# A two-stream encoder on one core: the last trailing chains on single PSUM banks, the sample's residual kept on chip through layer 1, and attention's turns cut differently

## The chip, the core and the metric

The kernel runs on one core of a Trainium2 chip. The core has a matrix engine (TensorE, PE in the profile), three element-wise engines (VectorE, DVE; ScalarE, ACT; GpSimd, POOL) and a queue that issues most transfers (SyncE, SP). TensorE writes its results into PSUM, eight banks of 128 partitions by 512 float32; the other operands lie in SBUF. The metric is device time of one execution in microseconds (us); lower is better.

## The reference

Two requests, the prompt (1024 tokens) and the sample (512 tokens), go through the same two layers of width 1024. Layer 0 mixes tokens with a grouped Fourier transform and a matrix, layer 1 with grouped-query attention (8 heads of 128, 2 key heads) with RMS-normed and rotated queries and keys. Each is followed by a SwiGLU of width 2816, and every step adds to a residual:

```python
for i in range(DEPTH):
    if i % 2 == 0:
        x = x + fourier_mixer(x, norm_mix[i], fourier_w[j])
    else:
        x = x + attention_mixer(x, norm_mix[i], attn_w_qkv[j], attn_q_norm[j],
                                attn_k_norm[j], attn_w_o[j], cos, sin)
    x = x + swiglu_ffn(x, norm_ffn[i], w_gate[i], w_up[i], w_down[i])
```

## The kernel before

**Blocks and precision.** Tokens stand in three blocks of 512: block 0 is the sample, blocks 1 and 2 the prompt. A residual block is eight tiles of 128 features by 512 tokens. Every product of two matrices is made of three matmuls (high by high, high by low, low by high part): `mm3`, lines 249 to 251, and `split` (lines 242 to 246) makes the two parts, a copy on ACT and a subtraction on DVE or POOL. One `mm3` on 512 columns is called a product below.

**Stages.** (1) The sample's Fourier layer. (2) The sample's SwiGLU of layer 0, woven with the prompt's Fourier layer. (3) `ffn_pair`: the prompt's SwiGLU of layer 0, both blocks at once in Strassen's manner. Behind its last round stand its trailing down products, which are issued in turns with the beginning of `main_1`. (4) `weave`: `main_1` (the sample's qkv, attention, out projection, norm and SwiGLU of layer 1) against `aux_2` (the prompt's qkv for block 2 and then block 1, its attention, its out projections, and `moving`, which prepares the operands of the last stage). (5) `ffn_pair` of layer 1, whose results go to the output `y`; its last trailing down products have nothing beside them.

**What sets the order.** The stages are Python generators. A `yield` carries a cost, and `weave` always continues the stream whose sum of costs, divided by its total, is smaller; so the costs only decide how two streams' instructions are mixed when they are written down. The Tile framework then schedules the written program with its own model of the engines and fixes one order for each engine and for the SP queue. On the chip each of them is first in, first out, and waits on semaphores.

**The trailing chains.** `product(k, d, f0)` (line 1034 on) is one product of the down matrix: `k` counts the seven Strassen products, `d` four output tiles. Four PSUM chains, one for each `d`, take products 0 to 3, then 4 and 5, then 6. After every product DVE adds the chain's running value to an accumulator (line 1054), so a chain's next product has to wait until that add has read the bank. In all rounds but the last a chain is one bank, from `bank()` or `bankg()`. In the last round (`f0 + 2 == NF`) of either layer it is one half of a tile of two banks (tag `gT`), which chains 0 and 1 share, and 2 and 3. The gate and up products of the same round use the same two `gT` tiles, one for each Strassen operand (`times`, line 1111 on).

**Sample's residual.** `accumulators()` takes two of the four 8 KB slots of the pool `accp`. In layer 1 the out projection (`linear_residual`, lines 744 to 755) loads a tile of the residual from DRAM into a temporary, adds the projection (line 752) and writes the sum back to DRAM (line 332). `normed` reads the eight tiles again (line 366), multiplies by the inverse norm on DVE (line 369) and splits them. `ffn` reads them a third time into accumulators it takes for itself (line 777). The prompt's attention uses the same pool: its transposed probabilities (`pt`) take two slots for a pair of query chunks.

**Attention.** `attend` goes over heads. For a query chunk `qc` of 128: `scores` (products into a `gX` tile, of which there is one, DVE's maximum on line 1346, ACT's exponential and scaling on lines 1350 and 1352); `turned` (eight transposes on PE, line 1364, split into `pt`); after every second chunk `values` (24 matmuls of 256 columns from `pt`). The prompt has eight chunks in a head, the sample four. The generator's yields stand between these steps.

Of the kernel before, what the change touches and what calls it, by code (L numbers as in the profile page):

```python
# [26 lines left out]
NF = DFF // P  # L27
# [98 lines left out]
def trunk_kernel(ctx: ExitStack, tc: tile.TileContext, t: dict):  # L126
# [59 lines left out]
    def tmp(n=TB, dt=F32):  # L186
        return tl("t", [n], dt, "t" + cur[0])
# [134 lines left out]
    def accumulators():  # L322
        halves = [acc_tile("acc", [4, TB], F32) for _ in range(2)]
        return [a[:, i] for a in halves for i in range(4)]
# [419 lines left out]
    def linear_residual(src, u, b, prev):  # L744

        for n in range(NC):
            w = weights(src[n])
            x = tmp()
            sp.dma_start(x, prev[:, n, :])
            ps = bank()  # L750
            project(w, u, ps)
            dve.tensor_tensor(x, ps, x, op=ALU.add)
            new_residual(b, n, x)
            yield 5.5


    kept, pend = {}, []

    def ffn(layer, b, h, out=None):
        h = h()  # L760
        here = b in resident
        acc = resident.pop(b) if here else accumulators()
        kept[b] = acc
        yield 0.0

        def halves(ms, wds, f0, dc):

            box = []

            def half(i):  # L770
                w = wds[dc // 4].rearrange("p h (f c) n -> p h f c n", f=2)
                mm3(box[0], w[:, 0, i, dc % 4], w[:, 1, i, dc % 4], ms[i][:, 0], ms[i][:, 1], i == 0, i == 1)

            def begin():
                box.append(bank())
                if f0 == 0 and not here:
                    sp.dma_start(acc[dc], xres[b][:, dc, :])
                half(0)

            def end():  # L780
                half(1)
                dve.tensor_tensor(acc[dc], box[0], acc[dc], op=ALU.add)  # L782
                if f0 + 2 == NF:
                    new_residual(b, dc, acc[dc], None if out is None else out[:, dc, :])

            return begin, end
# [135 lines left out]
    def ffn_pair(layer, blocks, ring, places, outs):  # L922
# [111 lines left out]
        def product(k, d, f0):  # L1034
# [8 lines left out]
            b, dc = blocks[c], 4 * o + d  # L1043
            acc = accs[b][dc]
            fresh, closes = k in (0, 4, 6), k in (3, 5, 6)
            if fresh and f0 + 2 < NF:
                chain[d] = bank() if d % 2 else bankg()
            elif fresh and d % 2 == 0:
                g2 = tl("a", [2, TB], F32, "gT", gt)
                chain[d], chain[d + 1] = g2[:, 0], g2[:, 1]  # L1050
# [254 lines left out]
    def attend(blocks, straight, slot):  # L1305
# [6 lines left out]
        for g in range(NKV):  # L1312
# [15 lines left out]
            for h in range(g * GROUP, (g + 1) * GROUP):  # L1328
# [49 lines left out]
                    act.copy(o, po[:, 0:256])  # L1378
                    sp.dma_start(dot[blocks[n]][:, h, c0 : c0 + 256], o)

                last = None
                for qc in range(nk + 1):
                    p = scores(qc) if qc < nk else None
                    yield 0.7 * nb
                    if qc:
                        turned(qc - 1, last)
                        yield 0.8 * nb
                        if qc % 2 == 0:
                            values(qc // 2 - 1)
                            yield 0.8 * nb  # L1390
                    last = p


    def weave(main, main_cost, aux=None, aux_cost=1.0, lead=0):
# [11 lines left out]
                runs.remove(run)  # L1406
        cur[0] = "F"

    FFN_US, PAIR_US, CHAIN_US, PROMPT_US = 352.0, 678.0, 223.0, 630.0

    mpt = open_pool("mp")
# [60 lines left out]

    def prepare(b, layer):

        yield from normed(b, g_ffn[layer], nxt, "A")

    def h_next():
        return nxt["h"]
# [49 lines left out]
    def out_projection(b, slot):  # L1528
        got = {}
        if b in mixed:  # L1530
            got["h"] = mixed.pop(b)
        else:
            yield from reloaded(dot[b], got, slot)
        yield from linear_residual(t["wo"], got["h"], b, xres[b])
# [6 lines left out]
    def main_1():  # L1541
        yield from qkv(0)
        yield from attend((0,), 0, "A")
        yield from out_projection(0, "A")
        yield from prepare(0, 1)
        yield from ffn(1, 0, h_next, t["y"][0])
# [128 lines left out]
```

## Time and profile before

| what | value |
|---|---|
| median of 3 runs | 2969.23 us (2968.76 to 2973.36) |
| the profiled execution: its time, its span | 2965.4 us, 2963.6 us |
| busy: PE, DVE, ACT, POOL | 2855.9, 1713.3, 1304.9, 1517.6 us |
| mean granted clock of TensorE | 0.99 |
| HBM read and written | 426.21 MB and 68.16 MB |
| direct transfers on SP's queue | 489.65 MB |

The profile is of one execution, and its times are counted from the span's start. A matmul's record is longer than its share of the pipeline: the pace of PE is read from one start to the next, not from a record's length. In a view of groups or of the timeline, a bracket or the part after the bar tells how long the engine had been idle before an instruction and which instruction of which engine ended the wait; PEld is the load of a matmul's stationary operand. "PEclk" is the clock that TensorE was granted, as a share of the full one.

### The profile page before, as it was taken

What the parts mean: (1) busy time and instruction counts of PE and PEld (TensorE: products, weight loads), DVE (VectorE), ACT (ScalarE), POOL (GpSimd) and SP (SyncE); (2) the same over time, 40 slices, a digit from 0 to 9 for tenths busy, and PEclk for the clock granted to TensorE, in tenths of its full rate; (3) what the DMA queues carried; (4) which work ended last, traced back from release to release, by engine and by line L of the source; (5) the groups of instructions that cost most, each with busy time, mean ns of one, the idle gap of its engine ahead of it and who ended that gap; (6) DMA issues with size and microseconds to landing.
All of it is one profiled execution on the core that took longest, in us unless ns stands there. A gap on an engine that the chain in (4) does not pass through costs nothing. (4 is left out here: it accounts for less than half of the span.)

```text
span 2963.6 us, 37198 instructions
## 1 busy us (share of the span) xinstructions
PE 2855.9 (96%) x13656; PEld 2350.0 (79%) x13656; DVE 1713.3 (58%) x3031; ACT 1304.9 (44%) x2131; POOL 1517.6 (51%) x932
## 2 busy tenths in 40 slices
PE   7999999999999999998998999999998999999998
PEld 6778878788888887786777888878886788888886
DVE  6674553566666667737646555552244466666666
ACT  5543232333333333646756776663333333333332
POOL 4344264766776774522241122224535767766763
PEclk8999999999999999999999999999999999999999
DMA  7435374766556553632242121115447865565552
GB/s 227 143 116 183 131 270 167 291 218 222 192 186 219 199 175 130 213 93 85 83 150 89 59 91 54 54 57 192 151 168 278 309 235 200 176 219 201 192 195 89
DMA packets 182326, 496.82 MB, mean 168 GB/s; under 512 B 19872, under 2 KB 30112, under 8 KB 180736
## 3 DMA queue, kind: packets, MB, share of 16 engines
q1 hardware_dynamic: 181216, 489.65, 48.5%
q0 software_dynamic: 640, 3.74, 0.4%
q8 instruction: 108, 1.77, 0.2%
q10 hardware_dynamic: 288, 1.05, 0.1%
q14 instruction: 74, 0.61, 0.1%
HBM read 426.21 MB, written 68.16 MB: 167 GB/s over the span
## 5 line engine op out<-in xcount | busy, mean ns | idle before, releaser
L288 POOL TENSOR_TENSOR w<-raw,w 128x1024 fp32r<-128x1024 f32 x200 | 479.0, 2402 | 843.9 <-ACT w L287 832.7
L243 POOL TENSOR_TENSOR w<-raw,w 128x512 fp32r<-128x512 f32 (+1 forms) x464 | 608.3, 1331 | 451.2 <-ACT w L242 445.0
L242 ACT CAST w<-raw 128x512 fp32r<-128x512 f32 (+1 forms) x464 | 279.6, 632 | 538.3 <-PE a L251 173.2
L287 ACT CAST w<-raw 128x1024 fp32r<-128x1024 f32 x200 | 208.7, 1049 | 269.5 <-PE g L251 77.9
L249 PE MATMUL g<-h,w 128*128 128x512 f32 x704 | 279.3, 397 | 9.9 <-ACT w L287 3.4
L251 PE MATMUL g<-h,w 128*128 128x512 f32 x704 | 277.8, 395 | 2.2 <-POOL w L288 2.2
L249 PE MATMUL a<-ring,w 128*128 128x512 f32 x712 | 279.5, 392 | 0.1
L251 PE MATMUL a<-ring,w 128*128 128x512 f32 x712 | 277.5, 390 | 0.0
L250 PE MATMUL a<-ring,w 128*128 128x512 f32 x712 | 277.3, 389 | 0.0
L250 PE MATMUL g<-h,w 128*128 128x512 f32 x704 | 276.8, 393 | 0.0
L1054 DVE TENSOR_TENSOR acc<-g,acc 128x512 f32<-128x512 f32 x280 | 192.5, 687 | 106.9 <-PE g L251 106.6
L1054 DVE TENSOR_TENSOR acc<-c,acc 128x512 f32<-128x512 f32 x280 | 192.4, 687 | 93.7 <-PE c L251 92.1
L249 PE MATMUL c<-mid,w 128*128 128x512 f32 x592 | 232.4, 393 | 13.3 <-ACT mid L242 7.6
L250 PE MATMUL c<-mid,w 128*128 128x512 f32 x592 | 232.6, 393 | 1.2 <-DVE mid L243 1.1
L251 PE MATMUL c<-mid,w 128*128 128x512 f32 x592 | 232.5, 393 | 1.3 <-POOL w L288 1.3
L249 PE MATMUL c<-h,w 128*128 128x512 f32 x480 | 191.5, 400 | 4.3 <-ACT h L245 3.3
L782 DVE TENSOR_TENSOR acc<-c,acc 128x512 f32<-128x512 f32 x176 | 120.9, 688 | 129.2 <-PE c L251 126.5
L250 PE MATMUL c<-h,w 128*128 128x512 f32 x480 | 189.1, 395 | 1.2 <-DVE h L246 0.9
L251 PE MATMUL c<-h,w 128*128 128x512 f32 x480 | 188.9, 394 | 0.0
L249 PEld LDWEIGHTS g<-h,w 128*128 128x128 f32 x704 | 133.0, 189 | 37.1 <-ACT w L287 3.8
L249 PEld LDWEIGHTS a<-ring,w 128*128 128x128 f32 x712 | 133.8, 188 | 33.8 <-DVE mid L243 4.4
L251 PEld LDWEIGHTS g<-h,w 128*128 128x128 f32 x704 | 132.9, 189 | 30.0 <-POOL w L288 3.3
(392 smaller groups left out, 6718.5 us busy)
## 6 DMA issues: line engine op xcount, KB each, us to landing
ring<-mov_B SPq DMA_DIRECT2D x248, 512.0 KB, 5.5
ring<-mov_T SPq DMA_DIRECT2D x88, 512.0 KB, 5.1
raw<-in_gate_dram SPq DMA_DIRECT2D x44, 512.0 KB, 3.6
raw<-in_up_dram SPq DMA_DIRECT2D x44, 512.0 KB, 3.5
raw<-in_down_dram SPq DMA_DIRECT2D x88, 256.0 KB, 3.1
raw<-in_gate_dram SPq DMA_DIRECT2D x88, 256.0 KB, 5.0
raw<-in_up_dram SPq DMA_DIRECT2D x88, 256.0 KB, 5.4
raw<-in_down_dram SPq DMA_DIRECT2D x44, 512.0 KB, 4.1
```

The costliest lines, as they stand in the source:

```text
L242: keep(act.copy(hi, src))
L243: keep(eng.tensor_tensor(lo, src, hi.bitcast(F32), op=ALU.subtract))
L249: pe.matmul(out, lh, rh, start=first, stop=False, **kw)
L250: pe.matmul(out, lh, rl, start=False, stop=False, **kw)
L251: pe.matmul(out, ll, rh, start=False, stop=last, **kw)
L287: pinned(act.copy(flat[:, 0], raw)) if early else act.copy(flat[:, 0], raw)
L288: pool.tensor_tensor(flat[:, 1], raw, flat[:, 0].bitcast(F32), op=ALU.subtract)
L782: dve.tensor_tensor(acc[dc], box[0], acc[dc], op=ALU.add)
L1054: dve.tensor_tensor(acc, chain[d], acc, op=ALU.add)
```

## The change

Three things are changed.

1. In the last round of layer 1, where `outs` is given, `product` takes single banks for its chains, as in the other rounds. Layer 0's last round keeps the `gT` halves, since the other stream is using the single banks by then.
2. `staying[0] = accumulators()` is taken before the sample's out projection. The residual is loaded straight into these tiles, stays there, is not written back, is read from there by `normed`, and is the accumulator of `ffn`. Eight writes (line 332) and sixteen reads (lines 366 and 777) of 256 KB leave SP's queue; the eight reads of line 749 remain. No engine other than SP has an instruction more or less.
3. `attend` yields at other places. The last turn of a head, which issues no scores, no longer yields 0.7. After the transposes of an even chunk it yields 2.0 (before 0.8), after those of an odd chunk 0.2 (before 0.8), after the values 0.2 (before 0.8), all times the number of blocks.

```diff
--- before.py
+++ after.py
@@ -745,21 +745,21 @@
 
         for n in range(NC):
             w = weights(src[n])
-            x = tmp()
+            x = staying[b][n] if b in staying else tmp()
             sp.dma_start(x, prev[:, n, :])
             ps = bank()
             project(w, u, ps)
             dve.tensor_tensor(x, ps, x, op=ALU.add)
-            new_residual(b, n, x)
+            new_residual(b, n, x, stays=b in staying)
             yield 5.5
 
 
-    kept, pend = {}, []
+    kept, pend, staying = {}, [], {}
 
     def ffn(layer, b, h, out=None):
         h = h()
         here = b in resident
-        acc = resident.pop(b) if here else accumulators()
+        acc = resident.pop(b) if here else staying[b]
         kept[b] = acc
         yield 0.0
 
@@ -773,8 +773,6 @@
 
             def begin():
                 box.append(bank())
-                if f0 == 0 and not here:
-                    sp.dma_start(acc[dc], xres[b][:, dc, :])
                 half(0)
 
             def end():
@@ -1043,7 +1041,7 @@
             b, dc = blocks[c], 4 * o + d
             acc = accs[b][dc]
             fresh, closes = k in (0, 4, 6), k in (3, 5, 6)
-            if fresh and f0 + 2 < NF:
+            if fresh and (f0 + 2 < NF or outs is not None):
                 chain[d] = bank() if d % 2 else bankg()
             elif fresh and d % 2 == 0:
                 g2 = tl("a", [2, TB], F32, "gT", gt)
@@ -1378,17 +1376,18 @@
                     act.copy(o, po[:, 0:256])
                     sp.dma_start(dot[blocks[n]][:, h, c0 : c0 + 256], o)
 
-                last = None
-                for qc in range(nk + 1):
-                    p = scores(qc) if qc < nk else None
-                    yield 0.7 * nb
-                    if qc:
-                        turned(qc - 1, last)
-                        yield 0.8 * nb
-                        if qc % 2 == 0:
-                            values(qc // 2 - 1)
-                            yield 0.8 * nb
-                    last = p
+                ps = []
+                for qc in range(nk + LAG):
+                    if qc < nk:
+                        ps.append(scores(qc))
+                        yield 0.7 * nb
+                    n = qc - LAG
+                    if n >= 0:
+                        turned(n, ps[n])
+                        yield (0.2 if n % 2 else 2.0) * nb
+                        if n % 2:
+                            values(n // 2)
+                            yield 0.2 * nb
 
 
     def weave(main, main_cost, aux=None, aux_cost=1.0, lead=0):
@@ -1406,6 +1405,7 @@
                 runs.remove(run)
         cur[0] = "F"
 
+    LAG = 1
     FFN_US, PAIR_US, CHAIN_US, PROMPT_US = 352.0, 678.0, 223.0, 630.0
 
     mpt = open_pool("mp")
@@ -1472,7 +1472,7 @@
 
     def prepare(b, layer):
 
-        yield from normed(b, g_ffn[layer], nxt, "A")
+        yield from normed(b, g_ffn[layer], nxt, "A", staying[b])
 
     def h_next():
         return nxt["h"]
@@ -1541,6 +1541,7 @@
     def main_1():
         yield from qkv(0)
         yield from attend((0,), 0, "A")
+        staying[0] = accumulators()
         yield from out_projection(0, "A")
         yield from prepare(0, 1)
         yield from ffn(1, 0, h_next, t["y"][0])
```

The rows below are the built order, with the tiles' numbers of each build. The first place is DVE near the program's end. `a_23702` (in the new order `a_23662`) is the `gT` tile with the last gate and up products, the Strassen operand N4; L1136, L1066 and L1084 turn it into the last operands, L243 splits them (`mid`, `ring`). The other rows are the adds of the trailing chains. Before:

```order
L1136 TENSOR_TENSOR a_23702<-a_23702,t_18974 128x512
L1054 TENSOR_TENSOR acc_18663<-a_23742,acc_18663 128x512
L1136 TENSOR_TENSOR a_23702<-a_23702,t_18975 128x512
L1066 TENSOR_TENSOR a_23702<-a_23702,t_18974 128x512
L1054 TENSOR_TENSOR acc_18663<-a_23742,acc_18663 128x512
L1084 TENSOR_TENSOR a_23702<-a_23702,f_18673 128x512
L1054 TENSOR_TENSOR acc_18665<-a_23742,acc_18665 128x512
L243 TENSOR_TENSOR mid_18672<-a_23702,mid_18672 128x512
L1054 TENSOR_TENSOR acc_18665<-a_23742,acc_18665 128x512
L243 TENSOR_TENSOR ring_18151<-a_23702,ring_18151 128x512
L1054 TENSOR_TENSOR acc_18666<-a_23742,acc_18666 128x512
L1054 TENSOR_TENSOR acc_18663<-a_23751,acc_18663 128x512
```

Now (line numbers are two lower from line 778 on):

```order
L1134 TENSOR_TENSOR a_23662<-a_23662,t_18934 128x512
L243 TENSOR_TENSOR mid_18613<-a_23619,mid_18613 128x512
L1052 TENSOR_TENSOR acc_18605<-g_23712,acc_18605 128x512
L1134 TENSOR_TENSOR a_23662<-a_23662,t_18935 128x512
L1052 TENSOR_TENSOR acc_18605<-c_23717,acc_18605 128x512
L1064 TENSOR_TENSOR a_23662<-a_23662,t_18934 128x512
L1052 TENSOR_TENSOR acc_18607<-g_23702,acc_18607 128x512
L1082 TENSOR_TENSOR a_23662<-a_23662,f_18615 128x512
L1052 TENSOR_TENSOR acc_18607<-c_23707,acc_18607 128x512
L1052 TENSOR_TENSOR acc_18607<-g_23712,acc_18607 128x512
L243 TENSOR_TENSOR mid_18614<-a_23662,mid_18614 128x512
L1052 TENSOR_TENSOR acc_18607<-c_23717,acc_18607 128x512
```

Before, the adds read one `gT` tile, `a_23742`, for eight products in a row, and only then the second, `a_23751`. Now they go round four banks, g, c, g, c, and two adds more stand ahead of the first row shown.

The second place is SP's queue about the end of the sample's out projection. `raw` are weights on their way in, `t` the sample's residual tiles, `dot` results of the prompt's attention. Before:

```order
L332 DMA xres_94<-t_13101 128x512
L283 DMA raw_13922<-in_down_dram 128x512 x2
L366 DMA t_13395<-xres_94 128x512
L1379 DMA dot_115<-t_13172 128x256
L332 DMA xres_94<-t_13202 128x512
L283 DMA raw_13983<-in_gate_dram 128x1024
L366 DMA t_13418<-xres_94 128x512
L366 DMA t_13423<-xres_94 128x512
L366 DMA t_13444<-xres_94 128x512
L366 DMA t_13449<-xres_94 128x512
L366 DMA t_13483<-xres_94 128x512
L366 DMA t_13488<-xres_94 128x512
```

Now:

```order
L1329 DMA raw_13691<-dqk_2_138 128x512
L1329 DMA raw_14191<-dqk_3_129 128x512
L1329 DMA raw_14191<-dqk_3_139 128x512
L283 DMA raw_13411<-in_up_dram 128x1024
L749 DMA acc_12395<-xres_94 128x512 x4
L283 DMA raw_13614<-in_gate_dram 128x1024
L283 DMA raw_13638<-in_up_dram 128x1024
L283 DMA raw_13844<-in_down_dram 128x512 x2
L1377 DMA dot_115<-t_13086 128x256
L1318 DMA raw_14715<-dqk_9_135 128x512
L1318 DMA raw_14715<-dqk_9_145 128x512
L283 DMA raw_13878<-in_gate_dram 128x1024
```

The residual's reads (L366) and the writes (L332) are gone from the queue, and what stood behind them has moved up. The second half of the staying residual (L749, four reads in one row) now stands behind the first loads of the SwiGLU's weights; the first half stands some 90 rows ahead, among the loads of the qkv weights.

The third place is DVE at the sample's norm, with the prompt's scores between (L1346, now L1344, is their maximum). Before:

```order
L1346 TENSOR_REDUCE col_13349<-a_13342 128x1 x2
L369 TENSOR_TENSOR g_13388<-c_13358,t_13390 128x512
L1347 SCALAR_TENSOR_TENSOR col_13349<-col_13349,nrqc 128x1
L243 TENSOR_TENSOR pt_13372<-c_13374,pt_13372 128x4x128
L243 TENSOR_TENSOR pt_13373<-c_13381,pt_13373 128x4x128
L369 TENSOR_TENSOR g_13389<-c_13358,t_13395 128x512
L1351 RECIPROCAL col_13353<-col_13353 128x1
L246 SCALAR_TENSOR_TENSOR h_13371<-g_13388,gains,h_13371 128x512
L246 SCALAR_TENSOR_TENSOR h_13371<-g_13389,gains,h_13371 128x512
L1346 TENSOR_REDUCE col_13407<-a_13400 128x1 x2
L369 TENSOR_TENSOR g_13416<-c_13358,t_13418 128x512
```

Now:

```order
L1344 TENSOR_REDUCE col_13246<-a_13239 128x1 x2
L243 TENSOR_TENSOR pt_13255<-c_13257,pt_13255 128x4x128
L1345 SCALAR_TENSOR_TENSOR col_13246<-col_13246,nrqc 128x1
L243 TENSOR_TENSOR pt_13256<-c_13264,pt_13256 128x4x128
L369 TENSOR_TENSOR g_13285<-c_13271,acc_12394 128x512
L369 TENSOR_TENSOR g_13286<-c_13271,acc_12394 128x512
L1349 RECIPROCAL col_13250<-col_13250 128x1
L246 SCALAR_TENSOR_TENSOR h_13284<-g_13285,gains,h_13284 128x512
L246 SCALAR_TENSOR_TENSOR h_13284<-g_13286,gains,h_13284 128x512
L1344 TENSOR_REDUCE col_13300<-a_13293 128x1 x2
L369 TENSOR_TENSOR g_13309<-c_13271,acc_12394 128x512
```

The norm's multiplications (L369) read `acc` and not `t`, and wait for no transfer. In the old order the last add of the out projection stands behind the maxima of 9 of the prompt's score steps, the eight L369 behind 12 and 13, and the first L852 of the SwiGLU behind 17; in the new one behind 8, 10 to 12, and 15. From the second L852 on the places agree within one step.

## The prediction

> **What bounds the kernel now.** I read the page's busy table first, then the busy time by stretches of the program, then the waits and the timeline of the stretches that lose time.
>
> ```profile
> span 2963.6 us, 37198 instructions
> PE 2855.9 (96%) x13656; PEld 2350.0 (79%) x13656; DVE 1713.3 (58%) x3031; ACT 1304.9 (44%) x2131; POOL 1517.6 (51%) x932
> ```
>
> PE is busy for 2855.9 of 2963.6 us. The change adds no work and takes none from PE, so it can only move the 107.7 us in which PE stands still, and the time in which its clock is lowered. The stretches say where these lie:
>
> ```profile
> core 0: us, PE busy (x) PEld busy (x) DVE busy (x) ACT busy (x) POOL busy (x), PEclk, DMA share, GB/s
> 1540.00:1605.00 65.00, 62.64 (x351) 52.57 (x349) 36.39 (x67) 41.27 (x61) 17.96 (x8) 0.98 0.33 114
> 1605.00:1640.00 35.00, 25.86 (x133) 22.05 (x133) 25.04 (x58) 22.05 (x37) 0.19 (x1) 0.85 0.20 61
> 1640.00:1700.00 60.00, 59.21 (x354) 50.41 (x353) 30.30 (x61) 45.55 (x65) 11.99 (x5) 1.00 0.21 68
> 1700.00:1850.00 150.00, 144.87 (x826) 122.50 (x825) 82.72 (x153) 103.30 (x144) 40.64 (x17) 1.00 0.22 72
> 1850.00:2000.00 150.00, 143.94 (x818) 121.06 (x817) 85.76 (x149) 101.70 (x144) 37.00 (x16) 1.00 0.17 54
> 2180.00:2310.00 130.00, 117.81 (x500) 94.37 (x499) 59.88 (x99) 44.97 (x69) 70.62 (x40) 0.95 0.71 254
> 2310.00:2920.00 610.00, 610.00 (x2678) 501.02 (x2678) 386.50 (x589) 217.31 (x390) 437.90 (x308) 1.00 0.60 208
> 2920.00:2964.00 44.00, 34.24 (x118) 21.41 (x116) 29.56 (x44) 7.30 (x13) 7.16 (x6) 0.91 0.26 96
> ```
>
> The last stage proper (2310 to 2920) has no idle PE at all. Three stretches that the change touches lose: the end (9.8 of 44 us, at clock 0.91), the sample's norm (1605 to 1640: 9.1 of 35, at 0.85), and the prompt's attention (5.1 and 6.1 of 150 each). `moving` (2180 to 2310: 12.2 of 130) is touched only through the order.
>
> **Term A, the trailing chains.** The last gate and up matmul starts at 2928.70; from there on the program is 28 products and 28 adds on DVE:
>
> ```profile
> 2926.21 0.39 PE L249 MATMUL a<-late,w 128*128 128x512 f32 x1
> 2926.44 0.39 PE L250 MATMUL a<-late,w 128*128 128x512 f32 x1
> 2928.70 0.39 PE L251 MATMUL a<-late,w 128*128 128x512 f32 x1
> 2930.86 0.51 PE L249 MATMUL a<-mid,w 128*128 128x512 f32 x1 [0.79 <-DVE acc L1054]
> 2932.87 0.47 PE L249 MATMUL a<-mid,w 128*128 128x512 f32 x1 [1.04 <-DVE acc L1054]
> 2940.60 0.63 PE L249 MATMUL a<-mid,w 128*128 128x512 f32 x1
> 2941.03 0.63 PE L250 MATMUL a<-mid,w 128*128 128x512 f32 x1
> ```
>
> ```profile
> 2929.13 0.70 DVE L1136 TENSOR_TENSOR a<-a,t 128x512 f32<-128x512 f32 x1
> 2930.11 0.69 DVE L1054 TENSOR_TENSOR acc<-a,acc 128x512 f32<-128x512 f32 x1 [0.28 <-PE a L251]
> 2930.72 0.69 DVE L1136 TENSOR_TENSOR a<-a,t 128x512 f32<-128x512 f32 x1
> 2931.44 0.70 DVE L1066 TENSOR_TENSOR a<-a,t 128x512 f32<-128x512 f32 x1
> 2936.39 0.68 DVE L243 TENSOR_TENSOR ring<-a,ring 128x512 fp32r<-128x512 f32 x1
> 2942.12 1.42 DVE L1054 TENSOR_TENSOR acc<-a,acc 128x512 f32<-128x512 f32 x2 [0.59 <-PE a L251]
> 2957.86 1.40 DVE L1054 TENSOR_TENSOR acc<-a,acc 128x512 f32<-128x512 f32 x2 [0.35 <-PE a L251]
> 2959.62 0.69 DVE L1054 TENSOR_TENSOR acc<-a,acc 128x512 f32<-128x512 f32 x1 [0.36 <-PE a L251]
> ```
>
> ```profile
> PEld a L249 <- DVE acc L1054: 9.6, 23, 1.2
> ```
>
> (The last row is of the waits: us in all, how many, the longest.) A matmul follows the one before in 0.227 us (2926.21 to 2926.44), so a product takes 0.68 us of PE. Yet the chain in the other half of a `gT` tile waits for the add that reads the first half: both waits go by tile, and a step costs product plus add plus their signals, 1.75 us. With one tile in turn that is the pace to about 2942; with two in turn 21 adds from 2942.12 to 2960.3 take 18.2 us, 0.87 each. With four single banks a chain's next product comes three products (2.0 us) after its last one ended, and finds its add of 0.69 done.
>
> What then limits? By the new order two of the 28 products go ahead of N4, into the hole of 1.25 us before its first matmul, so N4 still ends at 2929. *PE:* 26 products x 0.68 = 17.7, to 2946.7, and one add: 2947.6. *DVE:* from 2929.13 the order has 26 adds and 7 others (two L1136, L1066, L1084, three L243). Independent ones follow each other in 0.61 us (2930.11 to 2930.72): 33 x 0.61 = 20.1, and four dependent steps add 0.1 each (2930.72 to 2931.44 is 0.72): to 2949.6. *The operand:* the split into `ring`, which the fourth of the seven Strassen products needs, is the 14th of these 33, so it ends near 2929.1 + 14 x 0.62 = 2937.8; 16 products behind it take 10.9 and an add 0.9, to 2949.6 again. I take 2949.7 where the row has 2960.3: 10.6 less. The stretch from the last add to the span's end, 3.3 us, is the last output's transfer and stays. The 16 outputs now come in some 11 us:
>
> ```profile
> 2943.57 17.11 SPq L329 DMA_DIRECT2D out_y_dram<-acc  x16
> DMA to landing us min/median/max: 2.0/2.5/4.4
> ```
>
> If the last takes 4.4 and not 2.5 that costs 1.9; I take 0.6. **A = -10.0.** Bounds: PE alone sets the pace, -12.7; or all 33 DVE instructions take the 0.71 of the doubled rows (23.4, to 2952.5) and the slow clock below stays, -5.4.
>
> The clock: from 2936.6 to 2941.9 matmuls follow each other in 0.43 us (2940.60 to 2941.03), 12 of them, 2.4 us lost. It came after 7 us in which PE had one product of 0.68 in 1.75 us or more. In the new order PE has 12 products (8.2 us) in those 9 us, so I expect no drop. The Trainium skill, "TensorE: Matmul & The Clock Gate", section "HAM oscillation", gives as the rule that the clock stays up as long as no idle gap is longer than about 3.4 us; by that it would not have fallen here either, as no wait above is longer than 1.04, so the trace disagrees. By the rule A holds as summed; with the trace's drop repeated it would be 2.4 less.
>
> **Term B, the residual that stays.** Off the queue go 24 transfers of 256 KB. What they cost now:
>
> ```profile
> 1605.65 23.97 SPq L366 DMA_DIRECT2D t<-xres  x6
>   DMA t<-xres: 0.3, 1
> PE a L249 <- ACT p L1350: 6.1, 3, 2.5
> PE g L249 <- DVE h L246: 2.1, 1, 2.1
> ```
>
> SP is held up for 24 us by the reads, but DVE's L369 waited 0.3 us in all for one, and PE in that stretch waits for the exponential and for the norm's last split, not for weights. So the reads are hidden behind the norm's own work on DVE and ACT, which stays. What PE lacks there is the sample's work: between the last add of the out projection and the norm's end the built order has four score steps before and four after. I take 0. Upper bound: all 9.1 idle us of the stretch and up to 5 for its clock. The new costs: the first half of the tiles is loaded far ahead; the second half stands in SP's queue behind the loads of the first gate and up weights, which wait for a raw buffer. Late, it stops the fifth add, and with it the `bank()` of the seventh projection; two projections of 24 matmuls (2 x 5.4 us) and attention lie between, a landing takes 4.0 to 5.5 (L777 now), so 0. And `pt` has two slots from the start; that is the third rival.
>
> **Term C, the yields.** A pair of chunks still yields 3.8 per block. Work moves from behind the values to behind an even chunk's transposes, which would space the scores more evenly. But the scheduler had done that: at 0.227 us a matmul, the built orders have 19 (before) and 18 (now) of the 63 gaps between two score steps with under 4 us of other matmuls. The waits that it could end or double, outside 1605 to 1640:
>
> ```profile
> PE c L1364 <- ACT p L1352: 4.0, 3, 1.6
> PE a L249 <- ACT p L1350: 3.1, 4, 1.4
> ```
>
> That is 7.1 us either way, and I take 0. A head's total falls by 0.7 per block, so the sample's SwiGLU is written some 5 cost units later against `moving`, whose cover grows a little: 0.
>
> **Sum.** 2965.4 (the profiled execution) - 10.0 = 2955.4. The median of the runs shown is 3.8 us above that execution, 2969.2; so I forecast **2959**. With A between -12.7 and -5.4 and B and C within 3 it lies between 2953 and 2966.
>
> **The rivals.**
>
> *R1, more:* the norm's stretch shrinks too. For it: its reads take 24 us of SP, and loads come three at a time, so L369 may have been paced by them though DVE was never seen to wait. Against: the 0.3 us. Half of 14 us is 7: 2952.
>
> *R2, no difference that can be measured:* DVE's own pace with the slow clock, A = -5.4: 2964. Changes under 0.2% (6 us) can't be told from none here, so this is "same" unless B or C give a little. For it: nine rows show a DVE pair in 1.42. Against: they were spaced by PE, and single ones followed in 0.61.
>
> *R3, slower:* the prompt's attention starves on `pt`. Before, the sample's SwiGLU takes its two slots only here:
>
> ```profile
> 1541.14 1.29 DVE L1346 TENSOR_REDUCE col<-a 128x1 f32<-128x512 f32 x2 [3.73 <-PE a L251]
> 1685.25 0.69 DVE L1346 TENSOR_REDUCE col<-a 128x1 f32<-128x512 f32 x1
> 1689.53 1.81 SPq L777 DMA_DIRECT2D acc<-xres  x4
> 1695.60 0.29 PE L250 MATMUL c<-pt,w 128*128 128x256 f32 x1
> 1695.72 0.28 PE L251 MATMUL c<-pt,w 128*128 128x256 f32 x1
> ```
>
> From the first maximum to the 22nd, 11 pairs of chunks run with four slots; now with two, where the split of a pair's first transposes must wait for the values of the pair before, 24 matmuls x 0.115 = 2.75 us. Wholly exposed that is 30 us, two thirds exposed 20: 2979. It decides from 1.5 us a pair on (16 us eat A and 6 more). Against: from 1700 to 2000 the kernel before ran with two slots already, and lost 5.1 and 6.1 in 150 us, no more than the 2.4 in 65 with four.
>
> *That A does nothing* would need the chip and not the tile to order product and add; the tails of the other rounds, on single banks, run with PE never idle (2310 to 2920).
>
> **Chances.** Forecast 0.60, R1 0.14, R2 0.17, R3 0.09. Faster by over 0.2%: 0.57 + 0.14 + 0.04 = 0.75; within: 0.03 + 0.13 = 0.16; slower 0.09. The range for 8 in 10 takes in R2 and most of R1: 2949 to 2969.
>
> **What would show it.** In the profile after: from the last gate and up matmul to the last add some 21 us and not 31, DVE's adds 0.6 to 0.7 apart, no PE wait for L1052 over 0.5 us, clock 1.00 there. For B: the same hole of some 35 us with clock near 0.85 at the sample's norm, 8 to 10 us idle. For C: 4 to 7 us idle per 150 us of attention. Wrong it is if `moving` (12.2 idle now) changes by over 4, or if the splits into `pt` show waits for the values' matmuls.

## The result, and the profile after

The changed kernel took 2951.52 us (median of 4, 2951.06 to 2957.20) against 2968.99 us for the kernel before (median of 4, 2966.21 to 2973.36): a ratio of 0.9944, 95% interval 0.9927 to 0.9961. Beside a second, larger set of runs the ratio was 0.9956 (0.9942 to 0.9969). So it is faster, by 9 to 17 us in the second set. The forecast of 2959 was on the right side and its range held the time, but the gain was larger than the 10 us forecast. The profiled execution took 2951.21 us.

The head of the page of the changed kernel, and its stretches, to be held against those of before:

```profile
span 2949.4 us, 37141 instructions
PE 2848.6 (97%) x13656; PEld 2348.9 (80%) x13656; DVE 1714.1 (58%) x3031; ACT 1304.3 (44%) x2131; POOL 1517.4 (51%) x932
```

```profile
core 0: us, PE busy (x) PEld busy (x) DVE busy (x) ACT busy (x) POOL busy (x), PEclk, DMA share, GB/s
1540.00:1605.00 65.00, 59.14 (x340) 48.95 (x338) 41.29 (x86) 43.84 (x67) 15.26 (x7) 1.00 0.26 85
1605.00:1640.00 35.00, 29.74 (x160) 25.56 (x160) 21.15 (x41) 23.47 (x36) 2.39 (x1) 0.90 0.00 1
1640.00:1700.00 60.00, 57.84 (x344) 48.88 (x344) 34.66 (x66) 44.71 (x65) 13.25 (x6) 1.00 0.19 60
1700.00:1850.00 150.00, 142.67 (x805) 120.81 (x804) 84.38 (x149) 101.29 (x143) 36.97 (x17) 0.99 0.19 61
1850.00:2000.00 150.00, 144.73 (x838) 123.23 (x837) 86.09 (x151) 104.83 (x146) 40.27 (x17) 1.00 0.19 62
2180.00:2310.00 130.00, 116.35 (x490) 92.69 (x489) 56.20 (x85) 43.64 (x70) 71.97 (x41) 0.95 0.73 259
2310.00:2920.00 610.00, 610.00 (x2680) 501.12 (x2679) 391.73 (x595) 220.07 (x395) 439.77 (x309) 1.00 0.60 206
2920.00:2964.00 44.00, 22.63 (x94) 16.80 (x92) 22.87 (x37) 4.05 (x7) 3.80 (x3) 0.93 0.26 96
```

At the sample's norm (1605 to 1640) the transfers are gone (DMA share 0.00, before 0.20), the idle time of PE is 5.3 us instead of 9.1, and the clock 0.90 instead of 0.85. But the stretches beside it lose more than they did (5.9 and 2.2 us instead of 2.4 and 0.8): fixed windows cut a program that has moved by some microseconds at other places. A better ruler is PE's own order, since both kernels issue the same 13656 matmuls. From their start times in the traces I took how long PE needed from one matmul's number to another's; in brackets how many of these microseconds had the clock at half:

```
matmuls         0-2000     2000-7000   7000-7600   7600-8200  8200-9500  9500-10500 10500-13500  13500-last  to the end
before          395.8 (20) 1114.4 (3)  130.1 (14)  106.7 (0)  238.3 (0)  218.6 (0)  702.5 (14)   48.1 (7)    4.4
after           393.3 (14) 1114.1 (7)  125.1 (10)  109.1 (3)  237.4 (0)  218.7 (0)  703.3 (14)   37.3 (0)    6.6
```

The sample's norm lies in 7000 to 7600, the last trailing chains behind 13500. The two executions differ by 14.2 us: 10.8 less in the tail, 2.2 more between the last matmul and the end, 5.0 less at the norm of which 2.4 come back at once, and 2.5 less in the first 2000 matmuls, which no edit touches and where the clock was at half for 14 us instead of 20.

The tail, from the last gate and up matmul (2923.21) to the last product and add. First PE, then DVE:

```profile
2923.21 0.39 PE L251 MATMUL a<-late,w 128*128 128x512 f32 x1
2928.06 0.47 PE L249 MATMUL g<-mid,w 128*128 128x512 f32 x1 [0.30 <-DVE acc L1052]
2929.16 0.50 PE L249 MATMUL c<-mid,w 128*128 128x512 f32 x1 [0.17 <-DVE acc L1052]
2942.86 0.39 PE L251 MATMUL c<-mid,w 128*128 128x512 f32 x1
```

```profile
2923.64 0.70 DVE L1134 TENSOR_TENSOR a<-a,t 128x512 f32<-128x512 f32 x1 [1.03 <-PE a L251]
2930.22 0.68 DVE L1052 TENSOR_TENSOR acc<-c,acc 128x512 f32<-128x512 f32 x1
2931.42 0.68 DVE L243 TENSOR_TENSOR ring<-a,ring 128x512 fp32r<-128x512 f32 x1
2939.20 0.69 DVE L1052 TENSOR_TENSOR acc<-c,acc 128x512 f32<-128x512 f32 x1
2939.88 0.69 DVE L1052 TENSOR_TENSOR acc<-g,acc 128x512 f32<-128x512 f32 x1
2943.28 0.69 DVE L1052 TENSOR_TENSOR acc<-c,acc 128x512 f32<-128x512 f32 x1
```

From 2923.21 to the end of the last add, 2943.97, are 20.8 us; before there were 31.6 (2928.70 to 2960.31). DVE works without a gap from 2923.64 on, an instruction each 0.60 us; from 2939.2 on the adds stand 0.68 apart, which is PE's product. PE waits for an add only twice, for 0.3 and 0.2 us, and the clock stays at 1.00 (the 0.93 of the last stretch comes from half clock behind PE's last matmul).

### The profile page after: what moved, and what is told of

Its sections match the earlier page's. It is cut to its first block, busy times and chain, and to the rows that moved or that the text cites. A ratio compares the mean times of both kernels' runs of the same rounds, so it can differ in the third digit from the quotient of the medians.

```text
span 2949.4 us, 37141 instructions
## 1 busy us (share of the span) xinstructions
PE 2848.6 (97%) x13656; PEld 2348.9 (80%) x13656; DVE 1714.1 (58%) x3031; ACT 1304.3 (44%) x2131; POOL 1517.4 (51%) x932
## 4 chain that ended last, share of the span: by engine, by line
PE 41%; DVE 3%; issue 3%; ACT 2%; DMA 2%; POOL 2%; SPq 0%; POOLq 0%; ACTq 0%; DVEq 0%
PE a L249 6%; PE a L251 6%; PE a L250 6%; PE c L249 4%; PE c L250 4%; PE c L251 4%; PE g L251 3%; PE g L249 3%; PE g L250 3%; PE c L1362 2%; DVE col L1345 1%; POOL w L288 1%; DVE col L1344 1%; ACT p L1348 1%; ACT w L287 1%
## 5 line engine op out<-in xcount | busy, mean ns | idle before, releaser
L243 POOL TENSOR_TENSOR w<-raw,w 128x512 fp32r<-128x512 f32 (+1 forms) x464 | 608.5, 1332 | 436.5 <-ACT w L242 432.0
L1052 DVE TENSOR_TENSOR acc<-g,acc 128x512 f32<-128x512 f32 x294 | 201.7, 686 | 105.8 <-PE g L251 105.5
L1052 DVE TENSOR_TENSOR acc<-c,acc 128x512 f32<-128x512 f32 x294 | 201.6, 686 | 95.1 <-PE c L251 93.5
L249 PE MATMUL c<-mid,w 128*128 128x512 f32 x604 | 237.2, 394 | 17.0 <-ACT mid L242 8.9
L250 PE MATMUL c<-mid,w 128*128 128x512 f32 x604 | 236.2, 391 | 0.9 <-DVE mid L243 0.9
L251 PE MATMUL c<-mid,w 128*128 128x512 f32 x604 | 236.1, 391 | 0.7 <-POOL w L288 0.7
L780 DVE TENSOR_TENSOR acc<-c,acc 128x512 f32<-128x512 f32 x176 | 120.7, 688 | 118.8 <-PE c L251 118.1
```

The source lines that it names most:

```text
L243: keep(eng.tensor_tensor(lo, src, hi.bitcast(F32), op=ALU.subtract))
L249: pe.matmul(out, lh, rh, start=first, stop=False, **kw)
L250: pe.matmul(out, lh, rl, start=False, stop=False, **kw)
L251: pe.matmul(out, ll, rh, start=False, stop=last, **kw)
L1052: dve.tensor_tensor(acc, chain[d], acc, op=ALU.add)
```

## What the time of one execution is made of

The medians of the kernel before went from 2965.9 to 2969.0 between sets of runs, and its 74 executions beside the experiments from 2960.9 to 2973.7. They go with the mean granted clock: on average 2961.1 us at 0.992 and 2971.7 at 0.986. Over all 168 executions of the change, the kernel before and the experiments, a fit with one constant for each kernel and one slope gives 1.85 us for each 0.001 of clock, and leaves 1.6 us unexplained. I give both below: the ratio as measured, and "at equal clock" the constant of that fit against the kernel before, with two standard errors. The second is sharper, but leaves out what an edit does to the clock itself: the tail's stretch at half clock, 6.8 us long, is worth 0.0011 of mean clock, some 2 us. And the clock does go with the edits: the 40 executions of the four kernels in which a head's sum is smaller (the changed one, it without the tail, the yields alone, the last 0.7 left out alone) have a mean clock of 0.9899, the 97 of the kernel before, the tail alone and the residual alone 0.9884. By the slope that is 2.8 us, which "at equal clock" does not count.

For the changed kernel, ten executions: 9.2 us less at equal clock (plus or minus 1.1). Their median, 2953.1, is 13.4 below that of the 74, 2966.5; 3.7 us more go with the mean clock, 0.9904 against 0.9884, and how much of that the edit causes is not shown. The 17.5 between the first medians is more than the change: four executions at a mean clock of 0.991 stood against a kernel that runs at 0.9884 on average.

## Experiments

### The three parts apart

**The tail alone.**

```diff
# in the kernel before
-            if fresh and f0 + 2 < NF:
+            if fresh and (f0 + 2 < NF or outs is not None):
                 chain[d] = bank() if d % 2 else bankg()
```

> The kernel before with the single banks in the last trailing chains and nothing else. Theory 1 (the tail is the whole gain that the edit makes; the other 5.6 us that the two profiled executions differ by are 3.4 us of a shorter stretch of half clock at the start, which no edit touches, and small change in attention): 8 to 10 us less than before, of which PE and DVE end 10.8 us earlier after the last gate and up matmul and the last output's transfer gives 2.1 back. Theory 2 (the residual or the yields bring 5 to 8 us of their own): the same 8 to 10 here, and the rest is seen in the next three kernels. Theory 3 (the tail alone brings all 17.5, because the slow clock before it also goes): 15 or more.

2959.71 us (median of 12) against 2965.88 (median of 35): ratio 0.9979 (0.9970 to 0.9988), at equal clock 7.5 us less (plus or minus 1.0). In its trace matmuls 13500 to the last take 37.3 us, as in the changed kernel, and from there to the end it is 6.3 us. So the tail is worth some 6 to 9 us; theory 3, that it brings everything, falls.

**The other two parts without the tail.**

```diff
# in the changed kernel
-            if fresh and (f0 + 2 < NF or outs is not None):
+            if fresh and f0 + 2 < NF:
```

> The changed kernel with its last trailing chains put back on halves of the two-bank tiles; the residual and the yields stay changed. Theory 1: within 3 us of before. Theory 2: 5 to 8 us less than before. Rival R3 (two slots for the transposed probabilities starve the prompt's attention): more than before, with longer waits of PE in 1640 to 1700 us.

2965.08 us: ratio 0.9995 (0.9985 to 1.0005), at equal clock 0.3 less (plus or minus 1.0). The tail is back at 49.2 us, 10 of them at half clock. Theory 1 holds for the two together, and R3 does not: nothing starves.

**The residual alone.** The kernel before with `staying`, as in the diff of the change:

> The kernel before with the sample's residual kept in accumulators and nothing else. Theory 1: within 2 us of before, the hole at the sample's norm (9.1 us idle in 35, clock 0.85) as it was. Theory 2, if the norm's stage was paced by its reads after all: 4 to 7 us less, idle PE there 5 us or under and the clock above 0.9.

2965.37 us: ratio 0.9999 (0.9990 to 1.0008), at equal clock 0.9 less (plus or minus 1.0). The norm's stretch (7000 to 7600) takes 129.5 us against 130.1, and from 1605 to 1640 us PE idles for 7.7 us at a clock of 0.88. Taking 24 transfers off the queue moves nothing, and the two slots less for `pt` cost nothing.

**The yields alone.** The kernel before with the new loop of `attend`:

> The kernel before with the new yields in attention and nothing else. Theory 1: within 2 us of before. Theory 2, if the spacing of the scores mattered after all: 3 to 6 us less, seen as fewer waits for the scaled probabilities and the maximum in 1640 to 2000 us; but the sample's norm could then meet more or less of the other stream, 2 us either way.

2962.25 us: ratio 0.9990 (0.9978 to 1.0002), at equal clock 1.7 less (plus or minus 1.0). But the norm's stretch takes 125.3 us here, 5 less, and the next one 108.8, 2 more: it is the yields, not the residual, that change the norm's stretch in the changed kernel.

### Which half of the yields

The edit does two things: a head's sum falls by 0.7 (its last turn yields nothing), and the turns within a pair of chunks are spread otherwise. Each alone:

```diff
# yields_total: the new spread, with the last 0.7 kept
                     if qc < nk:
                         ps.append(scores(qc))
-                        yield 0.7 * nb
+                    yield 0.7 * nb
```

> The kernel before with the new spread of attention's yields, but a head's sum left as it was (the last turn still yields 0.7). In the four kernels with the new yields so far the stretch of matmuls 7000 to 7600, in which the sample's norm lies, takes 124.5 to 125.3 us against 129.5 to 130.1 in the three without; matmuls 7600 to 8200 then take 107.6 to 109.1 against 105.9 to 106.8, matmuls 8200 to 9500 take 237.3 against 238.3. Theory by position (the smaller sum of a head moves the norm against the scores, which is the gain): 129 to 131 in the norm's stretch here, and no gain over before. Theory by spread (the larger turn behind an even chunk's transposes is the gain): 124 to 126, and 1 to 4 us less than before.

```diff
# drop_last: the old spread, without the last 0.7
                     p = scores(qc) if qc < nk else None
-                    yield 0.7 * nb
+                    if qc < nk:
+                        yield 0.7 * nb
```

> The kernel before, where only the 0.7 of a head's last turn is left out of its yields, and the spread stays as it was. By position: 124 to 126 us in the norm's stretch (matmuls 7000 to 7600) and 1 to 4 us less than before. By spread: 129 to 131 there and no gain.

With the spread alone 2970.84 us against 2966.45: ratio 1.0018 (1.0007 to 1.0029), slower, by 3.7 us at equal clock (plus or minus 1.1). Without the last 0.7 alone 2959.12: ratio 0.9974 (0.9962 to 0.9986), 3.5 less at equal clock (plus or minus 1.3) and 7.3 by the medians. The norm's stretch takes 130.9 us with the spread and 123.5 without the 0.7: the theory by position, in both. In its one trace the spread alone loses behind the norm: matmuls 8200 to 9500 take 242.1 us for 238.3, 3.4 of them at half clock.

What the position changes is seen at the norm. The stretch from 1605 to 1650 us, of the kernel before, of the one without the 0.7, and of the one with the spread alone:

```profile
1605.00:1650.00 45.00, 35.86 (x196) 30.89 (x196) 29.41 (x67) 29.80 (x48) 0.19 (x1) 0.89 0.16 50
```

```profile
1605.00:1650.00 45.00, 38.62 (x221) 32.17 (x221) 29.27 (x55) 32.29 (x48) 7.11 (x3) 0.96 0.18 60
```

```profile
1605.00:1650.00 45.00, 35.85 (x169) 30.67 (x168) 27.70 (x62) 25.82 (x42) 2.36 (x1) 0.77 0.18 56
```

Busy PE is 35.9, 38.6 and 35.9 of 45 us, and the clock 0.89, 0.96 and 0.77. (Here too a fixed window is a rough ruler: matmul 7000 starts at 1514.9, 1512.8 and 1523.4 us.) In DVE's order the sample's last five out projection adds stand behind 2, 4, 6, 8 and 9 of the prompt's score steps before and with the spread alone, and behind 0, 2, 4, 6 and 8 without the 0.7; the norm's first multiplication stands behind 12 and behind 10. So the norm meets other work of the prompt. It is a few microseconds of waiting, and the clock counts them again: in the 45 us PE started 169 matmuls at 0.77 and 221 at 0.96. By matmul numbers this parts all the traces of this study: from 7000 to 7600 the clock is at half for 14 to 20 us in the four kernels with the old sum of a head, and for 3 to 11 us in the ten with the smaller one.

### The tail's mechanism

**Half of the chains on the shared tiles.**

```diff
# in the changed kernel: chains 2 and 3 take halves of a gT tile
-            if fresh and (f0 + 2 < NF or outs is not None):
+            if fresh and (f0 + 2 < NF or outs is not None and d < 2):
```

> The changed kernel, where in the last round chains 0 and 1 have single banks and chains 2 and 3 the two halves of one two-bank tile. Theory by tiles (a product waits until the add on the other half has read): chain 3 waits for chain 2's add in each of the seven rounds, about 1.07 us each less what DVE lacks anyway, so from the last gate and up matmul to the last add 24 to 28 us (31.6 before, 20.8 changed) and waits of PE for the add of 5 us or more. Rival (what cost the time was that these tiles were also wanted by the last gate and up sums, and not the sharing): 20.8 to 22, and waits under 2 us.

The time lies between the two ranges; the waits are the rival's. From the last gate and up matmul (2928.58) to the last add (2951.17) it is 22.6 us, 1.8 more than the changed kernel's 20.8, and nearly all of the loss stands in one place, ahead of the last product:

```profile
2947.68 0.40 PE L251 MATMUL a<-mid,w 128*128 128x512 f32 x1
2949.48 0.50 PE L249 MATMUL a<-mid,w 128*128 128x512 f32 x1 [1.40 <-DVE acc L1052]
2950.48 0.69 DVE L1052 TENSOR_TENSOR acc<-a,acc 128x512 f32<-128x512 f32 x1 [1.06 <-PE a L251]
```

The wait of a product for the add on its tile's other half is there: the product before it ends with the matmul of 2947.68, and the last one starts only at 2949.48, when DVE has read the other half. But with two chains on banks of their own the written order puts their products between those of the shared tile, and the wait is paid only where nothing is left to put there. So a shared tile does not by itself cost 10.8 us. How much of that was the sharing and how much that the last gate and up sums want the same two tiles, the traces separate in part. In the kernel before the last of these sums is read at 2936.39, and from 2942.12 on the chains have both tiles to themselves, at full clock: the last 21 adds take 18.2 us there, and 13.8 in the changed kernel (from 2930.22). These 4.4 us belong to the sharing by all four chains. The other 6.4 lie ahead of that, where the chains had one tile and the clock was at half for 6.8 us; there the causes stay mixed. The time, 2954.39 us (two executions; ratio 0.9955, 0.9937 to 0.9973), is too coarse to tell it from the changed kernel.

**Half of the output's bytes.**

```diff
# in the changed kernel, layer 1's last stage
-                new_residual(b, dc, acc, None if outs is None else outs[b][:, dc, :], room=spare, later=sums_of(b, dc), ends=(4, 3))
+                new_residual(b, dc, acc if outs is None else acc[:, 0:256],
+                             None if outs is None else outs[b][:, dc, 0:256], room=spare, later=sums_of(b, dc), ends=(4, 3))
```

> The changed kernel, where the last stage writes only the first half of the columns of each of its 16 last output tiles (and of the 8 that the sample does not write): half of the prompt's output is left out. If the transfers are the end's bound now (the DMA engines 0.95 to 0.98 busy and 354 to 363 GB/s from 2935 to 2945 us), the last transfer lands 2.0 to 3.3 us after the last add instead of 5.2, and the time falls by some 2 to 2.5 us. If not, that stays at about 5.

The stretches of the changed kernel and its 16 outputs on SP's queue, then this kernel; the last columns are the DMA engines' busy share and what they moved:

```profile
2935.00:2940.00 5.00, 5.00 (x24) 4.14 (x23) 5.00 (x10) 0.00 (x0) 0.00 (x0) 1.00 0.95 354
2940.00:2945.00 5.00, 3.24 (x15) 2.35 (x13) 3.97 (x6) 0.00 (x0) 0.00 (x0) 1.00 0.98 363
2934.51 10.17 SPq L329 DMA_DIRECT2D out_y_dram<-acc  x16
```

```profile
span 2951.2 us, 37141 instructions
2940.00:2945.00 5.00, 5.00 (x24) 4.14 (x23) 5.00 (x9) 0.00 (x0) 0.00 (x0) 1.00 0.66 221
2947.36 0.69 DVE L1052 TENSOR_TENSOR acc<-c,acc 128x512 f32<-128x512 f32 x1
```

With half the bytes the span ends 3.1 us after the last add (2948.05 to 2951.2); in the changed kernel it is 5.5 (2943.97 to 2949.4), in the kernel before it was 3.3. So the 16 outputs, which now come in 10.2 us instead of 17.1, fill the transfer engines, and the end has a new bound: 4.2 MB at 363 GB/s are 11.6 us. Single traces differ, though: from the last add to the end it is 3.3 to 4.5 us in the six traces with all chains on shared tiles (mean 3.9), and 4.1 to 5.9 in the six with all of them on single banks and all bytes written (mean 5.1). The 2.1 us between the first two is 1.2 over all. The Trainium skill, "Perfetto Trace Analysis", section "Roofline", says that a single core can go beyond its share of 358 GB/s up to some 435, where its 16 DMA engines end it; here these engines were 0.98 busy at 363, and the most that any trace shows for these writes in 5 us is 382 (the last kernel below), so by these traces the end comes earlier.

### The changed kernel again, and a better one

> The changed kernel once more, beside more executions of the kernel before. In the last set 35 executions of the kernel before ran from 2961.2 to 2973.7 us, the longer the lower their mean granted clock (0.992 to 0.986). Theory 1 (the edits are worth some 9 us, nearly all of it the tail; the 17.5 between the first medians came from few executions at unlike clocks): 7 to 11 us less than before here, with single executions from 2951 to 2965. Theory 2 (the three edits together give what no one of them gives alone): 14 us or more less again.

2955.62 us (median of 6, 2948.23 to 2960.00) against 2967.13 (median of 11): ratio 0.9956 (0.9942 to 0.9969). Its median is 11.5 below, just outside theory 1's 7 to 11, and at equal clock it is the same 9 us less as in the first set. The three parts alone sum to 10.1 at equal clock (7.5, 0.9 and 1.7), so nothing is left that only their joining would give.

**Turning two chunks later.** The loop of the change has a constant `LAG = 1`; for the prompt I made it two:

```diff
# in the changed kernel
-                for qc in range(nk + LAG):
+                lag = LAG * nb
+                for qc in range(nk + lag):
...
-                    n = qc - LAG
+                    n = qc - lag
```

> The changed kernel, where the prompt's attention turns a chunk's probabilities two chunks after its scores and not one; there are still two slots for the probabilities and one tile for the scores. If PE's waits in attention (5 to 7 idle us in 150) come from probabilities that are not ready for their transposes, 4 to 10 us less than the changed kernel. If they come from the one score tile, which the exponential frees, or if a chunk's probabilities wait for a slot, no change or up to 10 us more.

2946.89 us (median of 6, 2943.29 to 2949.50): ratio to before 0.9928 (0.9916 to 0.9940), which lies clear of the changed kernel's interval in the same set; 14.2 us less than before at equal clock (plus or minus 1.4), and 5.0 less than the changed kernel (plus or minus 1.7). PE's waits from 1645 to 1990 us, of the changed kernel and of this one (us in all, how many, the longest):

```profile
PE a L249 <- ACT p L1348: 5.7, 6, 2.2
PE c L1362 <- ACT p L1350: 3.1, 3, 1.5
PE c L249 <- DVE pt L243: 2.3, 2, 1.4
```

```profile
PE c L249 <- DVE pt L243: 4.6, 3, 1.7
PE a L249 <- ACT p L1348: 3.6, 3, 1.8
```

The transposes' wait for their probabilities (3.1 us) is gone, that for the score tile, which the exponential frees, shrinks, and the values wait more for the split of the transposes. Of these waits 2.9 us are gained; by matmul numbers the norm's stretch takes 122.2 us (125.1 in the changed kernel) and 8200 to 10500 take 452.0 (456.1).

> The kernel with the probabilities turned two chunks after their scores, which took 9 us less than the changed kernel, with a third slot for the probabilities. If a chunk's exponential still waits there for a slot that the transposes free, 2 to 6 us less than with two slots (2947) and fewer waits of PE for the exponential in 1645 to 1990 us (3.6 us in three). If the one score tile and the split of the transposes set what is left, within 2 us of it.

The edit is `"pX": 3` for 2. It took 2950.91 us: ratio 0.9949 (0.9935 to 0.9964), no gain; at equal clock 1.6 more than with two slots, inside the error (by the medians 4.0). PE's waits for the exponential stay, 3.5 us in three. The slot was not what is left.

```diff
# lag2_even: the kernel with lag 2, the old spread
-                        yield (0.2 if n % 2 else 2.0) * nb
+                        yield 0.8 * nb
                         if n % 2:
                             values(n // 2)
-                            yield 0.2 * nb
+                            yield 0.8 * nb
```

> The kernel that turns two chunks after the scores (2946.9 us), with the even spread of the kernel before in attention's yields (0.8, 0.8, 0.8 for 2.0 and 0.2, 0.2 and 0.2) and the head's smaller sum kept. If the new spread costs some 2 to 4 us (leaving out the last 0.7 alone took 7.3 us off the median, the new spread with it 3.6, the new spread without it added 4.4), 2 to 4 us less than with the new spread: 2943 to 2945. If the spread loses only where a chunk is turned right after the next one's scores, no difference over 2 us.

2954.02 us: ratio 0.9950 (0.9937 to 0.9962), at equal clock 6.1 more than with the new spread. The expectation was on the wrong side: the spread that loses with one chunk's lag (3.7 us with the old sum of a head, 1.8 with the smaller one) gains with two. Why is not settled; what differs by matmul numbers is 8200 to 9500 (238.7 against 235.3 us), the prompt's attention behind the norm. The best kernel of this study is thus the changed one with lag two, 2946.9 us.

## Why the prediction was right, and where it was wrong

**Term A: the mechanism and the sum were right, one part of it mis-sized.** 21.0 us were predicted from the last gate and up matmul to the last add, 20.8 were measured; DVE's pace set it, at 0.60 instead of 0.61, and in the last quarter PE's product of 0.68. The split into `ring` ended 8.9 us after the last gate and up matmul (2932.1; predicted 9.1 from the same point). The clock did not fall. What was mis-sized is the last transfer: 0.6 us were taken for outputs that come closer together, and between these two traces it was 2.1, above the 1.9 that stood as the bound (1.2 over all traces); the median landing rose from 2.5 us to 3.7:

```profile
DMA to landing us min/median/max: 2.0/3.7/5.0
```

The row that would have told it was in the trace of the kernel before, the last 5 us in which PE worked there:

```profile
2955.00:2960.00 5.00, 4.39 (x16) 2.43 (x15) 3.89 (x7) 0.00 (x0) 0.00 (x0) 1.00 0.80 300
```

With the outputs 1.1 us apart (16 in 17.11) the transfer engines were 0.80 busy at 300 GB/s, so full they would give some 375, an estimate; the 16 outputs of 262 KB ask for 381 in the 11 us forecast, and for 411 in the 10.2 that it took. A is then 8.7 us by the profile; by the runs of the tail alone it is 7.5 at equal clock and 6.2 by the medians.

**The clock in the tail.** The prediction set against the trace the rule of the Trainium skill that the clock stays up without an idle gap of some 3.4 us. The runs repeat that the rule does not hold here: of the six kernels with every chain on shared tiles all but one have a piece at half clock in the tail (us: before 7 us, the residual alone 7, the yields alone 3, without the 0.7 10, without the tail 10; none with the spread alone), and none with single banks for all of its chains, or for two, has. The same page of the Trainium skill, "TensorE: Matmul & The Clock Gate", has in the section "A second HAM failure mode: psum-queue depth-cycling" a case that comes nearer, of a bf16 kernel: short idle pauses between groups of matmuls, while it cycles through PSUM banks, with the clock falling and rising again. The trace agrees with that, with waits of 0.8 to 1.04 us, and that section was the one to weigh. But the kernel with the spread alone has the same waits without the fall, so what decides stays open.

**Term B: right.** 0 was predicted; 0.3 us less by the ratio, 0.9 at equal clock with an error of 1.0. That SP was held for 24 us cost nothing; the 0.3 us that DVE waited for a read was the row to go by. R3 fell: `pt` with two slots from the start costs nothing measurable, and the splits into `pt` wait for the transposes (27.4 us in all, of ACT, from 1605 to 2000) and nowhere for the values' matmuls.

**Term C: the step that failed.** The prediction argued that the scheduler had already spaced the scores evenly, so that the new spread would change nothing, "0", where the spread alone cost 3.7 us at equal clock; and that the smaller sum of a head only moves the sample's SwiGLU against `moving`, "0". That sum moves everything behind it, the norm first: the working had noted the places of the score steps around the norm and took equal counts for equal cost. It was worth 5 us in the norm's stretch and 3.5 at equal clock by itself, of which the new spread takes back 2; the clock that goes with it comes on top. Through it the sign given for B failed too, though B itself is right: "the same hole of some 35 us with clock near 0.85" is not what came, 5.3 idle us at 0.90 did. R1 had the right place, the norm's lean stage, and the wrong cause, the reads.

For the rest of attention 4 to 7 idle us in 150 were expected, and 7.3 and 5.3 came.

**R2** fell: DVE's adds did not keep the 0.71 of the doubled rows. `moving` idled for 13.7 us instead of 12.2, within the 4 allowed.

**The sum and the level.** That the 9.2 us at equal clock stand so near the forecast 10 is luck in part: A, put at 10.0, brought some 1 to 4 less, and C, put at 0, brought 1.7 at equal clock and 3.0 with its clock (the yields alone). That 17.5 us stood between the first medians and not 10 is in part the norm's clock, in part chance. The tail's clock, though it no longer falls there, does not show in the mean clock of the tail alone (0.9884, as before). The forecast set its 10 us off from the median of three executions, 2969.2, where 74 later ones have 2966.5, and one execution of this kernel is uncertain by 6 us either way, because of the clock alone.

## What to carry to other kernels

Where a stage that makes outputs is sped up, price the outputs' bytes at the rate that the trace shows as its highest, over the shorter time: the transfer that was hidden becomes the end. A change of a cost that only decides how two streams are mixed is priced at every place behind it where one stream is lean, not where the edit stands; each half of such an edit can have its own sign. And before medians that differ by half a per cent are compared, hold the granted clock of each execution beside its time.

## What was not expected of the hardware

The time of one and the same program varied by 12 us and more (2948.2 to 2960.0 for the changed kernel, 2960.9 to 2973.7 for the one before) with its mean clock, 1.85 us for 0.001. The stretches at half clock came in multiples of 3.41 us in all twelve traces of the experiments and in both of the two kernels, apart from the piece that the end of the span cuts off. The longest lies in the first 60 us, where PE is busy for 43 us in the kernel before, and differed most between executions: from 14 us in ten of the traces to 31 in two, with nothing changed there.
